# Moving the blocks of a weight tile in SBUF: two encoder layers on one Trainium2 core

## The chip, the cores and the metric

The kernel runs on one core of one Trainium2 chip. The metric is the device time of one execution in microseconds. The runs of the kernel before took 2366.05, 2366.12 and 2366.2 us; the median is 2366.12 us.

## The reference: what is computed

Two layers of a bidirectional encoder act on 272 rows (256 tokens and 16 learned meta tokens) of 2048 features, all in float32. Cut to what matters here, one layer is:

```python
proj = jnp.einsum('bld,dp->blp', h, w_in)                     # 2048 -> 6176 columns
y_gla = _gla_mixer(gq, gk, gv, gr, glr, gla_w_up, ...)        # chunkwise gated linear attention, both directions
y_na = _na_mixer(nq, nk, nv, na_rel_bias)                     # 2-D neighbourhood attention with 16 heads
mix = jnp.einsum('blm,md->bld', jnp.concatenate([y_gla, y_na], axis=-1), w_out)
h = _layer_norm(DEEPNORM_ALPHA * h + mix, ln1_w, ln1_b)
ff = jnp.einsum('blf,fd->bld', jnp.square(jax.nn.relu(jnp.einsum('bld,df->blf', h, w_ff1))), w_ff2)
h = _layer_norm(DEEPNORM_ALPHA * h + ff, ln2_w, ln2_b)        # w_ff1: 2048 -> 8192, w_ff2: 8192 -> 2048
```

The meta tokens are dropped at the end, so the second layer computes most things for 256 rows only. Nearly all arithmetic is in the four dense products with `w_in`, `w_out`, `w_ff1` and `w_ff2`.

## The kernel before, in words

**Numbers in two parts.** TensorE multiplies operands in the format fp32r, which holds less than float32. So each operand is kept as a high part (the value rounded to fp32r) and a low part (the rest). A product w·x is computed as three matmuls: high w on high x, high w on low x, low w on high x.

**Activations.** They lie with features on the 128 partitions and tokens along the free dimension, 16 tiles for x, 16 for y, and 32 for the hidden layer u (the first 16 of these reuse the place of y). `pair` makes one tile of 2 x 288 numbers for both parts. In the first layer the high part has 272 columns from the start of the tile, and the low part begins at number 288 (`PITCH`), which is 1152 bytes on. In the second layer ("dense") the two parts of 256 columns lie back to back in y and u, so that one matmul can stream both as 512 columns (`once`).

**Weights.** They come from memory in 768 tiles of 128 x 1024 numbers, each of them eight blocks of 128 x 128. `order` fixes the order of all 768, and `weights` keeps two tiles made ahead. `made` issues the load on the queue of SP, then lets ScalarE (ACT) round the tile to its high part `wh` (L180) and VectorE (DVE) subtract to get the low part `wl` (L181). Three buffers each of `raw`, `wh` and `wl` are in turn. The first tile of all is loaded and split in pieces by `head`.

**Matmuls.** `by_m` walks over the output blocks; for each it takes tiles of eight weight blocks and calls `eight`: eight times high weights on the high and on the low part (L216, 272 columns each, or L213, both parts at once as 512 columns), then eight times low weights on the high part (L219). Each matmul has its own weight load, which runs beside the matmul ahead of it. `by_k` (L246) is used in a few places where the inputs become ready one after another: it holds four or eight output banks open and gives each weight block of a tile to another of these.

**What else runs.** Attention, normalisation and evictions are generators that are stepped between weight tiles (`pump`). Their matmuls stand between those of the dense products: among them GLA's outputs (L638 to L642), whose stationary blocks are from `V` and whose streamed operand is `parts`, a tile of rows of 272 numbers.

**Addresses.** A weight tile is 4096 bytes per partition and each block of it 512 bytes. The tiles of x, y, u and the weights all begin at multiples of 256 bytes in a partition, which the unused tile `pad` of 40 numbers at the head of the constants brings about. A block of weights therefore begins at a multiple of 256 bytes from any high part, and 128 bytes off that from any low part of the first layer.

Of the kernel before, what the change touches and what calls it, by code (L numbers as in the profile page):

```python
# [7 lines left out]
F32 = mybir.dt.float32  # L8
F32R = mybir.dt.float32r
U8 = mybir.dt.uint8  # L10
AF = mybir.ActivationFunctionType
ALU = mybir.AluOpType
PSUM = bass.MemoryType.PSUM

P = 128
D = 2048
DC = D // P
T = 256
NM = 16
L = T + NM  # L20
# [6 lines left out]
WB = 1024  # L27
# [10 lines left out]
MEET = 2  # L38
PAD = 40
PITCH = 288  # L40


class Pair(tuple):


    def __new__(cls, both, dense=False):
        flat = both.rearrange("p a c -> p (a c)")
        parts = (flat[:, :T], flat[:, T:2 * T]) if dense else (both[:, 0, :], both[:, 1, :])
        made = super().__new__(cls, parts)
        made.both, made.once = both, flat[:, :2 * T] if dense else both[:, :, :T]  # L50
        return made


class Trunk:
    def __init__(self, ctx, tc, ins, out):
        self.ctx, self.tc, self.nc = ctx, tc, tc.nc
        self.i, self.out = ins, out
        self.bg, self.fg, self.credit, self.fcredit = deque(), deque(), 0, 0
        self.wants, self.due, self.late = {}, None, 0
        self.x = [None] * DC  # L60
        self.stream, self.ready = self.order(), deque()
        pool = lambda name, **k: ctx.enter_context(tc.tile_pool(name=name, **k))
        self.cp = pool("const", bufs=1)
        self.xp = pool("xhl", bufs=1)
        self.yp = pool("yhl", bufs=1)
        self.wp = pool("wst", bufs=3)
        self.jp = pool("jn", bufs=1)
        self.pm = pool("pm", bufs=4, space=PSUM)
        self.pb = pool("pb", bufs=4, space=PSUM)
# [102 lines left out]
    def made(self, ap, ends):  # L172
        if ap is None:
            return None
        nc = self.nc
        raw, wh, wl = (self.wp.tile([P, WB], d, name=nm, tag=nm)
                       for nm, d in (("raw", F32), ("wh", F32R), ("wl", F32R)))
        for c in map(slice, (0,) + ends, ends):
            nc.sync.dma_start(raw[:, c], ap[:, c])
            nc.scalar.copy(wh[:, c], raw[:, c])  # L180
            self.wl = nc.vector.tensor_tensor(wl[:, c], raw[:, c], wh[:, c].bitcast(F32), ALU.subtract).ins  # L181
        if not ends:
            self.head(ap, raw, wh, wl)
        return wh, wl

    def head(self, ap, raw, wh, wl):

        nc, q = self.nc, WB // 4
        both = self.xr.tile([P, 2, q + L], F32, name="head", tag="head", bufs=1)
        self.x[:2] = [self.pair(self.xp, "x", c) for c in range(2)]  # L190
        for c in range(2):
            nc.sync.dma_start(both[:, c], self.i["head"][:, c])
        nc.sync.dma_start(raw[:, 2 * q:], ap[:, 2 * q:])
        for c in range(2):
            at = slice(c * q, c * q + q)
            h, lo = (t[:, :L] for t in self.x[c])
            todo = [(both[:, c, q:], h, lo), (both[:, c, :q], wh[:, at], wl[:, at])]
            for args in todo[::-1] if c else todo:
                self.split(*args)
        for at in (slice(2 * q, 3 * q), slice(3 * q, WB)):  # L200
            nc.scalar.copy(wh[:, at], raw[:, at])
            self.wl = nc.vector.tensor_tensor(wl[:, at], raw[:, at], wh[:, at].bitcast(F32), ALU.subtract).ins

    def eight(self, ps, wh, wl, x, n, first, last, once):

        mm = self.nc.tensor.matmul
        c = lambda w, j: w[:, j * P:j * P + P]  # L210
        for j, v in enumerate(x):
            if once:
                mm(ps, lhsT=c(wh, j), rhs=v.once, start=first and not j, stop=False)  # L213
                continue
            for i in range(2):
                mm(ps[:, :n], lhsT=c(wh, j), rhs=v[i][:, :n], start=first and not i + j, stop=False)  # L216
        o = ps[:, T:] if once else ps[:, :n]
        for j, (h, _) in enumerate(x):
            mm(o, lhsT=c(wl, j), rhs=h[:, :T if once else n], start=False, stop=last and j == 7)  # L219
# [10 lines left out]
    def by_k(self, acts, n, before, wide=False):  # L230

        ps = [self.pm.tile([P, 512], F32, name="mm", tag="mm") for _ in range(4)]
        if wide:
            ps += [self.bank() for _ in range(4)]
        nk = len(acts)
        for k in range(0, nk, 2):
            before(k)
            for g in range(0, len(ps), 4):
                wh, wl = self.weights()
                parts = ((wh, 0), (wh, 1), (wl, 0))  # L240
                order = [(j, p, m) for j in range(2) for p in range(3) for m in range(4)]
                by_output = k == nk - 2 or k == 0 and not wide
                order.sort(key=lambda o: (o[0], o[2] // 2) if wide and not k + g else (by_output and o[2], o[1] // 2))
                for j, p, m in order:
                    c = j * 512 + m * P
                    self.nc.tensor.matmul(ps[g + m][:, :n], lhsT=parts[p][0][:, c:c + P], rhs=acts[k + j][parts[p][1]][:, :n],  # L246
                                          start=k + j + p == 0, stop=k == nk - 2 and j + p == 3)
        return [p[:, :n] for p in ps]

# [26 lines left out]

    def pair(self, pool, name, c):
        both = pool.tile([P, 2, PITCH], F32R, name=f"{name}{c}", tag=f"{name}{c}", bufs=1)
        return Pair(both, dense=name in ("y", "u") and not self.full)


    def layer(self, l):
# [91 lines left out]
    def load_gates(self):  # L374

        place = lambda c: self.yp.tile([P, 2, PITCH], F32, name=f"gw{c}", tag=f"y{c}", bufs=1).rearrange("p a c -> p (a c)")[:, :512]
        *self.wup, self.wlr = (place(c) for c in (8, 9, 10))
# [563 lines left out]
    def reuse(self, name, c, dtype):  # L941

        t = self.xp.tile([P, 2, PITCH], dtype, name=f"{name}{c}", tag=f"x{c}", bufs=1)
        return t.rearrange("p a c -> p (a c)")[:, :512]
# [235 lines left out]
```

## Time and profile before

| what | value |
|---|---|
| median of the runs | 2366.12 us |
| the profiled execution | 2366.29 us |
| its span, from the first to the last instruction | 2364.5 us |
| mean granted TensorE clock | 0.999 |
| TensorE busy | 2356.2 us (100%) |
| weight loads busy | 2241.9 us (95%) |
| VectorE busy | 1520.8 us (64%) |
| ScalarE busy | 1219.3 us (52%) |
| read from memory | 414.03 MB, 176 GB/s over the span |

"Busy" of TensorE is measured from each matmul's start to its modelled end. Matmuls overlap, since one begins while the one ahead of it still drains, so the sum of the durations in a group is more than the time in which they passed. The rate at which they follow each other is read from the timeline: the start of one group, the start of the next, and the number of matmuls between.

### The profile page before, as it was taken

What the parts mean: (1) busy time and instruction counts of PE and PEld (TensorE: products, weight loads), DVE (VectorE), ACT (ScalarE), POOL (GpSimd) and SP (SyncE); (2) the same over time, 40 slices, a digit from 0 to 9 for tenths busy, and PEclk for the clock granted to TensorE, in tenths of its full rate; (3) what the DMA queues carried; (4) which work ended last, traced back from release to release, by engine and by line L of the source; (5) the groups of instructions that cost most, each with busy time, mean ns of one, the idle gap of its engine ahead of it and who ended that gap; (6) DMA issues with size and microseconds to landing.
All of it is one profiled execution on the core that took longest, in us unless ns stands there. A gap on an engine that the chain in (4) does not pass through costs nothing.

```text
span 2364.5 us, 44607 instructions
## 1 busy us (share of the span) xinstructions
PE 2356.2 (100%) x18180; PEld 2241.9 (95%) x18180; DVE 1520.8 (64%) x2432; ACT 1219.3 (52%) x2100; POOL 136.2 (6%) x200
## 2 busy tenths in 40 slices
PE   9999999999999999999999999999999999999998
PEld 9999999999999999999999899999988888888888
DVE  5588777775544455546576787778766455666654
ACT  5666664564433344444456666655644333444443
POOL 0021100100000000000030111101100000000000
PEclk9999999999999999999999999999999999999999
DMA  7454445555555555555555555455566666556664
GB/s 261 153 160 153 156 135 176 173 176 178 177 178 176 176 177 179 177 177 174 177 184 171 164 160 165 155 160 188 187 192 190 189 187 188 188 190 212 195 188 144
DMA packets 118301, 419.02 MB, mean 177 GB/s; under 512 B 13512, under 2 KB 14024, under 8 KB 118096
## 3 DMA queue, kind: packets, MB, share of 16 engines
q1 hardware_dynamic: 117808, 415.65, 55.8%
q8 instruction: 142, 2.33, 0.4%
q14 instruction: 63, 0.52, 0.1%
q10 hardware_dynamic: 288, 0.52, 0.1%
HBM read 414.03 MB, written 2.10 MB: 176 GB/s over the span
## 4 chain that ended last, share of the span: by engine, by line
PE 98%; DVE 1%; issue 0%; ACT 0%; POOL 0%; DVEq 0%; ACTq 0%; POOLq 0%
PE mm L216 35%; PE mm L219 29%; PE mm L213 22%; PE mm L246 6%; PE bg L246 1%; PE bg L757 1%; PE mm L696 1%; PE bg L557 0%; PE bg L403 0%; DVE wl L181 0%; PE mm L722 0%; PE mm L446 0%; PE bg L883 0%; PE bg L608 0%; PE bg L638 0%
## 5 line engine op out<-in xcount | busy, mean ns | idle before, releaser
L181 DVE TENSOR_TENSOR wl<-raw,wh 128x1024 fp32r<-128x1024 f32 (+1 forms) x768 | 941.8, 1227 | 621.5 <-ACT wh L180 618.4
L180 ACT CAST wh<-raw 128x1024 fp32r<-128x1024 f32 (+1 forms) x768 | 803.5, 1047 | 919.4 <-PE mm L216 367.7
L216 PE MATMUL mm<-x,wh 128*128 128x272 f32 (+2 forms) x4224 | 569.8, 287 | 0.0
L216 PEld LDWEIGHTS mm<-x,wh 128*128 128x128 f32 x4224 | 541.1, 188 | 0.8 <-PE mm L696 0.2
L219 PE MATMUL mm<-x,wl 128*128 128x272 f32 (+3 forms) x3264 | 466.9, 285 | 0.0
L219 PEld LDWEIGHTS mm<-x,wl 128*128 128x128 f32 x3264 | 437.5, 189 | 11.6
L213 PE MATMUL mm<-x,wh 128*128 128x512 f32 x1152 | 290.1, 394 | 0.0
L213 PEld LDWEIGHTS mm<-x,wh 128*128 128x128 f32 x1152 | 207.2, 189 | 37.9 <-PE mm L696 0.4
L219 PE MATMUL mm<-y,wl 128*128 128x272 f32 (+1 forms) x1408 | 200.5, 285 | 0.0
L219 PEld LDWEIGHTS mm<-y,wl 128*128 128x128 f32 x1408 | 189.5, 189 | 6.5
L216 PE MATMUL mm<-y,wh 128*128 128x272 f32 (+1 forms) x1440 | 193.3, 286 | 0.0
L216 PEld LDWEIGHTS mm<-y,wh 128*128 128x128 f32 x1440 | 184.3, 188 | 0.0
L213 PE MATMUL mm<-y,wh 128*128 128x512 f32 x688 | 172.6, 392 | 0.0
L219 PE MATMUL mm<-u,wl 128*128 128x272 f32 (+1 forms) x1024 | 145.8, 285 | 0.0
L213 PEld LDWEIGHTS mm<-y,wh 128*128 128x128 f32 x688 | 123.6, 189 | 21.9
L219 PEld LDWEIGHTS mm<-u,wl 128*128 128x128 f32 x1024 | 137.8, 189 | 4.8
L216 PE MATMUL mm<-u,wh 128*128 128x272 f32 (+1 forms) x1056 | 141.2, 286 | 0.0
L216 PEld LDWEIGHTS mm<-u,wh 128*128 128x128 f32 x1056 | 134.9, 188 | 0.0
L213 PE MATMUL mm<-u,wh 128*128 128x512 f32 x496 | 124.2, 392 | 0.0
L213 PEld LDWEIGHTS mm<-u,wh 128*128 128x128 f32 x496 | 89.2, 189 | 15.9
L246 PE MATMUL mm<-x,wh 128*128 128x272 f32 (+1 forms) x512 | 73.3, 288 | 0.0
L246 PEld LDWEIGHTS mm<-x,wh 128*128 128x128 f32 x512 | 67.9, 191 | 0.0
(273 smaller groups left out, 1856.5 us busy)
## 6 DMA issues: line engine op xcount, KB each, us to landing
raw<-in_wff SPq DMA_DIRECT2D x512, 512.0 KB, 3.6
raw<-in_win SPq DMA_DIRECT2D x190, 512.0 KB, 3.8
raw<-in_wout SPq DMA_DIRECT2D x64, 512.0 KB, 3.6
nb<-in_nab SPq DMA_DIRECT2D x16, 352.0 KB, 4.7
xraw<-in_xT SPq DMA_DIRECT2D x7, 272.0 KB, 5.2
out<-out SPq DMA_DIRECT2D x5, 256.0 KB, 3.2
brow<-in_norm SPq DMA_DIRECT2D x4, 256.0 KB, 4.8
gw<-in_wup SPq DMA_DIRECT2D x4, 196.0 KB
```

The source lines that it names most:

```text
L180: nc.scalar.copy(wh[:, c], raw[:, c])
L181: self.wl = nc.vector.tensor_tensor(wl[:, c], raw[:, c], wh[:, c].bitcast(F32), ALU.subtract).ins
L213: mm(ps, lhsT=c(wh, j), rhs=v.once, start=first and not j, stop=False)
L216: mm(ps[:, :n], lhsT=c(wh, j), rhs=v[i][:, :n], start=first and not i + j, stop=False)
L219: mm(o, lhsT=c(wl, j), rhs=h[:, :T if once else n], start=False, stop=last and j == 7)
L246: self.nc.tensor.matmul(ps[g + m][:, :n], lhsT=parts[p][0][:, c:c + P], rhs=acts[k + j][parts[p][1]][:, :n], start=k + j + p == 0, stop=k ...
L696: nc.tensor.matmul(ps[hh][:, t * NKEY:t * NKEY + NKEY], lhsT=q[hs, NM + t * P:NM + t * P + P], rhs=k[hs, t, :], start=True, stop=True)
L757: nc.tensor.matmul(po[t][hs, :P], lhsT=v2[ts, hs] if rest else v1[:, t, hs], rhs=p2[ts, hh, :] if rest else p1[:, 2 * hh + t, :], start=re ...
```

## The change

The eight blocks of `wh` and of `wl` no longer lie back to back. Between the starts of two blocks lie 128 numbers plus a skew of 0, 8, ..., 56 numbers, that is 0 to 224 bytes of gap. The skew of a high tile is `SKEWS[(t + t // 8) % 8]` for the t-th weight tile, that of a low tile `SKEWS[t // 8 * 3 % 8]`, so 64 tiles in a row meet all 64 pairs. Each of these tiles takes 1472 numbers (5888 bytes) per partition rather than 1024. The copy of ScalarE and the subtraction of VectorE are the same, but write eight rows of 128 numbers. The low part of u in the first layer begins 1088 bytes behind its high part for u16 to u23 and 1216 bytes behind for u24 to u31, rather than 1152. The scratch space for dynamic DMAs goes from 8192 to 2048 bytes, which makes room. Numbers, order and count of the matmuls and weight loads stay as they are.

```diff
+SKEWS = (0, 8, 16, 24, 32, 40, 48, 56)
+SPAN = 1472
 class Pair(tuple):
-    def __new__(cls, both, dense=False):
+    def __new__(cls, both, dense=False, low=PITCH):
         flat = both.rearrange("p a c -> p (a c)")
-        parts = (flat[:, :T], flat[:, T:2 * T]) if dense else (both[:, 0, :], both[:, 1, :])
+        parts = (flat[:, :T], flat[:, T:2 * T]) if dense else (flat[:, :L], flat[:, low:low + L])
+        if low == PITCH and not dense:
+            parts = both[:, 0, :], both[:, 1, :]
...
-        raw, wh, wl = (self.wp.tile([P, WB], d, name=nm, tag=nm)
-                       for nm, d in (("raw", F32), ("wh", F32R), ("wl", F32R)))
+        raw = self.wp.tile([P, WB], F32, name="raw", tag="raw")
+        blocks = raw.rearrange("p (b c) -> p b c", c=P)
+        wh, wl = (self.skewed(nm, s) for nm, s in zip(("wh", "wl"), self.skew()))
         for c in map(slice, (0,) + ends, ends):
             nc.sync.dma_start(raw[:, c], ap[:, c])
-            nc.scalar.copy(wh[:, c], raw[:, c])
-            self.wl = nc.vector.tensor_tensor(wl[:, c], raw[:, c], wh[:, c].bitcast(F32), ALU.subtract).ins
+            self.halves(blocks, wh, wl, slice(c.start // P, c.stop // P))
...
+    def skew(self):
+        t = self.tiles
+        self.tiles += 1
+        return SKEWS[(t + t // 8) % 8], SKEWS[t // 8 * 3 % 8]
+
+    def skewed(self, name, skew):
+        flat = self.wp.tile([P, SPAN], F32R, name=name, tag=name)
+        return bass.AP(flat.tensor, flat.offset, [flat.ap[0], [P + skew, WB // P], [1, P]])
+
+    def halves(self, raw, wh, wl, at):
+        self.nc.scalar.copy(wh[:, at], raw[:, at])
+        self.wl = self.nc.vector.tensor_tensor(wl[:, at], raw[:, at], wh[:, at].bitcast(F32), ALU.subtract).ins
...
-        c = lambda w, j: w[:, j * P:j * P + P]
+        c = lambda w, j: w[:, j]
...
-                    c = j * 512 + m * P
-                    self.nc.tensor.matmul(ps[g + m][:, :n], lhsT=parts[p][0][:, c:c + P], rhs=acts[k + j][parts[p][1]][:, :n],
+                    self.nc.tensor.matmul(ps[g + m][:, :n], lhsT=parts[p][0][:, 4 * j + m], rhs=acts[k + j][parts[p][1]][:, :n],
...
     def pair(self, pool, name, c):
         both = pool.tile([P, 2, PITCH], F32R, name=f"{name}{c}", tag=f"{name}{c}", bufs=1)
-        return Pair(both, dense=name in ("y", "u") and not self.full)
+        low = PITCH if name != "u" else L if c < 24 else 2 * PITCH - L
+        return Pair(both, dense=name in ("y", "u") and not self.full, low=low)
...
-    nc = bacc.Bacc("TRN2", target_bir_lowering=False, num_devices=1, dynamic_dma_scratch_size=8192)
+    nc = bacc.Bacc("TRN2", target_bir_lowering=False, num_devices=1, dynamic_dma_scratch_size=2048)
```

More of the change, by code (lines that the diff above doesn't have):

```diff
@@ L60, in __init__ @@
         self.x = [None] * DC
-        self.stream, self.ready = self.order(), deque()
+        self.stream, self.ready, self.tiles = self.order(), deque(), 0
         pool = lambda name, **k: ctx.enter_context(tc.tile_pool(name=name, **k))
@@ L175, in made, with head @@
         nc = self.nc
-        raw, wh, wl = (self.wp.tile([P, WB], d, name=nm, tag=nm)
-                       for nm, d in (("raw", F32), ("wh", F32R), ("wl", F32R)))
+        raw = self.wp.tile([P, WB], F32, name="raw", tag="raw")
+        blocks = raw.rearrange("p (b c) -> p b c", c=P)
+        wh, wl = (self.skewed(nm, s) for nm, s in zip(("wh", "wl"), self.skew()))
         for c in map(slice, (0,) + ends, ends):
             nc.sync.dma_start(raw[:, c], ap[:, c])
-            nc.scalar.copy(wh[:, c], raw[:, c])
-            self.wl = nc.vector.tensor_tensor(wl[:, c], raw[:, c], wh[:, c].bitcast(F32), ALU.subtract).ins
+            self.halves(blocks, wh, wl, slice(c.start // P, c.stop // P))
         if not ends:
-            self.head(ap, raw, wh, wl)
+            self.head(ap, raw, blocks, wh, wl)
         return wh, wl
-    def head(self, ap, raw, wh, wl):
+    def skew(self):
[8 more added lines that the diff above has]
+        self.wl = self.nc.vector.tensor_tensor(wl[:, at], raw[:, at], wh[:, at].bitcast(F32), ALU.subtract).ins
+    def head(self, ap, raw, blocks, wh, wl):
         nc, q = self.nc, WB // 4
@@ L194, in head @@
         for c in range(2):
-            at = slice(c * q, c * q + q)
+            at = slice(2 * c, 2 * c + 2)
             h, lo = (t[:, :L] for t in self.x[c])
-            todo = [(both[:, c, q:], h, lo), (both[:, c, :q], wh[:, at], wl[:, at])]
+            todo = [(both[:, c, q:], h, lo), (both[:, c, :q].rearrange("p (b c) -> p b c", c=P), wh[:, at], wl[:, at])]
             for args in todo[::-1] if c else todo:
                 self.split(*args)
-        for at in (slice(2 * q, 3 * q), slice(3 * q, WB)):
-            nc.scalar.copy(wh[:, at], raw[:, at])
-            self.wl = nc.vector.tensor_tensor(wl[:, at], raw[:, at], wh[:, at].bitcast(F32), ALU.subtract).ins
+        for at in (slice(4, 6), slice(6, 8)):
+            self.halves(blocks, wh, wl, at)
     def eight(self, ps, wh, wl, x, n, first, last, once):
         mm = self.nc.tensor.matmul
-        c = lambda w, j: w[:, j * P:j * P + P]
+        c = lambda w, j: w[:, j]
         for j, v in enumerate(x):
```

## The prediction

> **What bounds the kernel now.** I read the page's busy times first, then the chain that ended last, then who waited for whom, then the groups by shape, and last the timeline of TensorE, for the distance from one matmul's start to the next. From the page:
>
> ```profile
> span 2364.5 us, 44607 instructions
> PE 2356.2 (100%) x18180; PEld 2241.9 (95%) x18180; DVE 1520.8 (64%) x2432; ACT 1219.3 (52%) x2100; POOL 136.2 (6%) x200
> PE 98%; DVE 1%; issue 0%; ACT 0%; POOL 0%; DVEq 0%; ACTq 0%; POOLq 0%
> PE mm L216 35%; PE mm L219 29%; PE mm L213 22%; PE mm L246 6%; PE bg L246 1%; PE bg L757 1%; PE mm L696 1%; PE bg L557 0%; PE bg L403 0%; DVE wl L181 0%; PE mm L722 0%; PE mm L446 0%; PE bg L883 0%; PE bg L608 0%; PE bg L638 0%
> L181 DVE TENSOR_TENSOR wl<-raw,wh 128x1024 fp32r<-128x1024 f32 (+1 forms) x768 | 941.8, 1227 | 621.5 <-ACT wh L180 618.4
> L180 ACT CAST wh<-raw 128x1024 fp32r<-128x1024 f32 (+1 forms) x768 | 803.5, 1047 | 919.4 <-PE mm L216 367.7
> ```
>
> TensorE is the chain, 98% of the span, 86% of it in three lines of one function. All its waits, from the view of waits:
>
> ```profile
> PE bg L372 <- DVE zero L369: 1.2, 1, 1.2
> PE bg L883 <- ACT sp L268: 0.7, 1, 0.7
> PE bg L883 <- DVE sp L269: 0.3, 1, 0.3
> ```
>
> That is 2.2 us, so no engine feeds it too late. The time is the number of matmuls times the pace at which one follows another. How many there are, by shape:
>
> ```profile
> L216 PE MATMUL mm<-x,wh 128*128 128x272 f32 x3584 | 483.1, 287 | 0.0
> L216 PE MATMUL mm<-y,wh 128*128 128x272 f32 x1408 | 189.1, 286 | 0.0
> L216 PE MATMUL mm<-u,wh 128*128 128x272 f32 x1024 | 137.1, 286 | 0.0
> L219 PE MATMUL mm<-x,wl 128*128 128x272 f32 x1792 | 260.3, 287 | 0.0
> L219 PE MATMUL mm<-y,wl 128*128 128x272 f32 x704 | 102.3, 287 | 0.0
> L219 PE MATMUL mm<-u,wl 128*128 128x272 f32 x512 | 74.4, 287 | 0.0
> L213 PE MATMUL mm<-x,wh 128*128 128x512 f32 x1152 | 290.1, 394 | 0.0
> L213 PE MATMUL mm<-y,wh 128*128 128x512 f32 x688 | 172.6, 392 | 0.0
> L213 PE MATMUL mm<-u,wh 128*128 128x512 f32 x496 | 124.2, 392 | 0.0
> L219 PE MATMUL mm<-x,wl 128*128 128x256 f32 x1152 | 160.4, 282 | 0.0
> L219 PE MATMUL mm<-y,wl 128*128 128x256 f32 x704 | 98.2, 282 | 0.0
> L219 PE MATMUL mm<-u,wl 128*128 128x256 f32 x512 | 71.4, 282 | 0.0
> ```
>
> 6016 matmuls with high weights over 272 columns, 3008 with low weights over 272, 2336 over 512 and 2368 over 256. The durations overlap; the pace is in the timeline of TensorE (first column: start in us):
>
> ```profile
> 821.73 2.14 PE L216 MATMUL mm<-u,wh 128*128 128x272 f32 x16
> 823.71 1.16 PE L219 MATMUL mm<-u,wl 128*128 128x272 f32 x8
> 824.71 2.14 PE L216 MATMUL mm<-u,wh 128*128 128x272 f32 x16
> 1900.92 2.00 PE L213 MATMUL mm<-u,wh 128*128 128x512 f32 x8
> 1902.76 1.12 PE L219 MATMUL mm<-u,wl 128*128 128x256 f32 x8
> 1903.71 2.00 PE L213 MATMUL mm<-y,wh 128*128 128x512 f32 x8
> ```
>
> One tile of layer 0 takes 16 matmuls in 1.98 us (123.8 ns each), then 8 in 1.00 us (125 ns). One of layer 1 takes 8 in 1.84 us (230 ns), then 8 in 0.95 us (118.8 ns). The grouped durations lie 162 ns above these paces (286 against 123.8, 392 against 230), so a duration in the other rows is read as a pace by taking 162 off. Times counts, the four groups make 744.5 + 376.0 + 537.3 + 281.2 = 1939 us of the span.
>
> **Part 1: weight blocks at other distances.** Nothing is added or removed on TensorE: the same matmuls and weight loads stand in the same order. What changes is the address at which a weight block begins against the operand that streams past. Before, every weight block, every high part and every second-layer low part begins at a multiple of 256 bytes from the others; a low part of x, y or u in layer 0 lies 1152 bytes behind its high part, so 128 bytes off. After, the high tile takes one of eight distances by its number and the low tile another, by its number over 8. In the built program the high-weight matmuls over 272 columns, half of them at 0 and half at 128 before, then stand at 0 and 128 in about a quarter of the cases each, and at 32, 64, 96, 160, 192, 224 in the rest. One tile in eight keeps its old distance, so 7/8 of the matmuls of by_m can change pace.
>
> Does the trace hold matmuls at such distances? The GLA outputs do: their streamed operand (parts) has rows of 1088 bytes and starts 160 past a multiple of 256, and V blocks lie at 512, so the distances there are 32, 96, 160 and 224. The first row and the row after the last of seven plus seven of them over 272 columns, and the same over 256:
>
> ```profile
> 145.54 0.28 PE L638 MATMUL bg<-parts,V 128*128 128x272 f32 x1
> ...
> 147.30 0.91 PE L216 MATMUL mm<-x,wh 128*128 128x272 f32 x6
> ```
>
> ```profile
> 1506.60 0.28 PE L639 MATMUL bg<-parts,V 128*128 128x256 f32 x1
> ...
> 1508.14 1.04 PE L216 MATMUL mm<-x,wh 128*128 128x272 f32 x7
> ```
>
> 14 matmuls in 1.76 us are 125.7 ns each; 13 in 1.54 us are 118.5 ns each. And those of by_k in layer 0, at 0 and 128 but four in a row with one operand:
>
> ```profile
> 26.43 2.18 PE L246 MATMUL bg<-x,wh 128*128 128x272 f32 x16
> 28.44 1.17 PE L246 MATMUL bg<-x,wl 128*128 128x272 f32 x8
> ```
>
> 16 in 2.01 us, 125.6 ns. So 125.6 to 125.7 is the pace over 272 columns wherever the steady exchange of a high and a low part at 0 and 128 is missing, whatever the distances. That exchange is the one row that is quicker (123.8), and the change breaks it in seven tiles of eight. I take 125.7.
>
> The sum, each count times 7/8: high weights over 272, 6016 x 7/8 x (125.7 - 123.8) = +10.0 us; low weights over 272, 3008 x 7/8 x (125.7 - 125.0) = +1.8 us; over 256, 2368 x 7/8 x (118.5 - 118.8) = -0.6 us. Over 512 columns no other distance is in the trace. Its bounds are the quickest and slowest undisturbed rows of that line, and those of the other two lines stand beside it (minimum, median, maximum in ns):
>
> ```profile
> L213 PE MATMUL mm<-u,wh x496: 389/391/398, 1819.9 to 2338.6; 128*128 128x512 f32 x166
> L216 PE MATMUL mm<-u,wh x1056: 283/288/290, 642.9 to 2350.3; 128*128 128x272 f32 x171, 128*128 128x256 f32 x5
> L219 PE MATMUL mm<-u,wl x1024: 277/284/296, 644.9 to 2351.2; 128*128 128x272 f32 x86, 128*128 128x256 f32 x85
> ```
>
> The mean of 392 lies near the minimum, 3 ns above 389 and 6 below 398, so most of these run in the line's quick state; the x rows at 394 carry 320 matmuls whose streamed operand has a gap of 128 bytes in its middle. I take half the way to x, +1 ns: 2336 x 7/8 x 1 = +2.0 us. The remaining matmuls (L246, small ones) are left at their rows. Sum: +13 us.
>
> **Part 2: low part of u.** It lies 1088 bytes behind the high part for u16 to u23, 1216 for u24 to u31, 64 bytes off the old 1152 either way. Only the 1024 high-weight matmuls on u over 272 columns see it, and only the tiles with unmoved weights are not yet counted: 1024 / 8 x 1.9 ns = 0.2 us.
>
> **Part 3: the split.** ACT's copy and DVE's subtraction now run over 8 rows of 128 instead of one of 1024. Per tile they are 1047 and 1227 ns; DVE is idle for 621.5 us before its 768, ACT for 919.4, so each could grow by 0.8 us per piece before it set the pace. Cost nil, hidden beside the 2.8 to 3.0 us that TensorE spends on a tile; without the cover a tenth more per piece would be 94 us of DVE time. Bounds: zero below, a few tenths of a microsecond above, in the first 50 us where TensorE follows the loads. The scratch space that shrinks from 8192 to 2048 bytes moves all tiles by 6144 bytes, a multiple of 256, and no queue of the page uses it: nil.
>
> **The sum.** 2366.3 us for the profiled execution (0.2 above the median of 2366.1) + 13 + 0.2 = 2379; I say 2380. Lower end, every line at the minima above (216: 283, low weights over 272: 283, low weights over 256: 277, 512 columns: 389): 7/8 x (-3.3 x 6016 - 4 x 3008 - 5 x 2368 - 3 x 2336) = -44 us, 2322. Upper end, at the 290 of L216, 4 ns on the low weights (L416's mean below), 3 ns over 256, 398 over 512: 7/8 x (4 x 6016 + 4 x 3008 + 3 x 2368 + 6 x 2336) = +50 us, 2416.
>
> ```profile
> L416 PE MATMUL bg<-lr,up 98*128 98x272 f32 x16 | 3.4, 291 | 0.0
> L403 PE MATMUL bg<-x,ws 128*64 128x272 f32 x32 | 8.1, 286 | 0.0
> ```
>
> L416 (distance 64) and L403 (32 and 160, with a shorter weight load) are the other rows at such distances: one worse, one like today's.
>
> **The rivals.** *Faster:* the two streams collide most where their blocks stand in step, and the spread takes them apart. For it: pace differs by address at all (283 to 290 in one shape). Against it: the GLA rows at spread distances are no quicker. It would give L216 a pace of 121 (its quicker half), low weights 121, 512 columns 227: 7/8 x (-2.8 x 6016 - 4 x 3008 - 3 x 2336) = -31 us, 2335. It decides once the mean over 272 columns falls under 123.8 ns. Chance 0.27.
>
> *No difference:* the streams don't disturb each other, the spread of durations is pipeline jitter, and the address does nothing: 2366. Against it stands the regularity of the rows above: by_m's 123.8 and by_k's 125.6 differ only in order and address. Chance 0.11. The Trainium skill has this as a rule: TensorE: Matmul & The Clock Gate, Step-by-step, says that two independent read ports let the next weights load without taking from the running matmul, and SBUF — State Buffer, Who interferes with whom, that TensorE waits on no one. By it the sum would be 2366 instead of 2380; the trace here leans against it.
>
> *Worse than forecast:* some of the 64 pairings run at the slow rows (290, 398) and nothing falls back into step, so the mean goes half-way to the upper end, +25 us and more, 2391 to 2416. For it: L416 and the 134 ns steps inside L219 (296). Chance 0.17.
>
> The first of those pages, Wait — 56ns, not 53.3ns?, gives N/2.4 + 2.5 ns for a warm matmul, 116 ns over 272 columns and 216 over 512; as an estimate by that, the most a perfect layout could give is some 75 us over 272 and 33 over 512. No row of this kernel runs at it.
>
> **How the numbers follow.** The forecast, 2380 (2371 to 2391), has 0.45. A measurement of this kernel tells about 0.2% from no change, 4.7 us. Faster by more: the first rival, 0.27, and a hair of the jitter. Within: the second and the lowest end of the forecast, 0.13. Slower: 0.60. The range of 8 in 10 reaches from the faster rival's 2335 to 2412, just inside the upper end.
>
> **What would show it.** TensorE still at 98% of the chain and the waits still near 2 us: then only pace moved. L216 (L232 after) over 272 columns near 288 instead of 286.5, L219 (L235) over 272 near 287.5, over 256 unchanged, L213 (L229) near 394. Wrong if the 272 groups fall under 286, or if DVE or ACT shows up as a releaser of TensorE.

## The result and the profile after

The changed kernel takes 2376.82 us in the median (2376.53 to 2376.88), the kernel before 2366.16 us over the runs of both rounds. The ratio is 1.0043, with a 95% interval of 1.0029 to 1.0057: slower by 10.7 us. The profiled execution has a span of 2375.0 us against 2364.5 us, 10.5 us more, and the clock is the same (1.00).

From the page of the kernel after, its busy line and the engines of its chain, and from its view of waits, everything that TensorE waited for:

```profile
PE 2366.8 (100%) x18180; PEld 2247.2 (95%) x18180; DVE 1520.0 (64%) x2432; ACT 1219.2 (51%) x2100; POOL 135.6 (6%) x200
PE 99%; DVE 0%; DMA 0%; ACT 0%; issue 0%; SPq 0%; DVEq 0%; ACTq 0%
```

```profile
PE bg L388 <- DVE zero L385: 1.2, 1, 1.2
PE bg L899 <- ACT sp L283: 0.7, 1, 0.7
PE bg L899 <- DVE sp L284: 0.3, 1, 0.3
```

TensorE is still the whole chain, the counts are the same, and its waits are the same 2.2 us. The split on VectorE and ScalarE takes what it took (1520.0 and 1219.2 us). So all of the 10.5 us is pace. The groups by shape of the kernel after, in the order of the prediction's (L232 is L216 of before, L235 is L219, L229 is L213):

```profile
L232 PE MATMUL mm<-x,wh 128*128 128x272 f32 x3584 | 487.5, 288 | 0.0
L232 PE MATMUL mm<-y,wh 128*128 128x272 f32 x1408 | 191.1, 288 | 0.0
L232 PE MATMUL mm<-u,wh 128*128 128x272 f32 x1024 | 138.7, 288 | 0.0
L235 PE MATMUL mm<-x,wl 128*128 128x272 f32 x1792 | 261.4, 288 | 0.0
L235 PE MATMUL mm<-y,wl 128*128 128x272 f32 x704 | 102.8, 288 | 0.0
L235 PE MATMUL mm<-u,wl 128*128 128x272 f32 x512 | 74.8, 288 | 0.0
L229 PE MATMUL mm<-x,wh 128*128 128x512 f32 x1152 | 291.9, 395 | 0.0
L229 PE MATMUL mm<-y,wh 128*128 128x512 f32 x688 | 173.9, 394 | 0.0
L229 PE MATMUL mm<-u,wh 128*128 128x512 f32 x496 | 125.2, 394 | 0.0
L235 PE MATMUL mm<-x,wl 128*128 128x256 f32 x1152 | 159.6, 281 | 0.0
L235 PE MATMUL mm<-y,wl 128*128 128x256 f32 x704 | 97.5, 281 | 0.0
L235 PE MATMUL mm<-u,wl 128*128 128x256 f32 x512 | 71.0, 281 | 0.0
```

The first number after the bar is the busy time of a group, and its difference to before is where the time went: high weights over 272 columns 4.4 + 2.0 + 1.6 = +8.0 us; low weights over 272 +1.1 + 0.5 + 0.4 = +2.0 us; over 512 columns +1.8 + 1.3 + 1.0 = +4.1 us; over 256 columns -0.8 - 0.7 - 0.4 = -1.9 us. That is +12.2 us; the other groups give 1.7 us back, by_k 0.8 of it.

The timeline of TensorE of the kernel after shows the pace of single tiles:

```profile
815.12 2.17 PE L232 MATMUL mm<-u,wh 128*128 128x272 f32 x16
817.12 1.16 PE L235 MATMUL mm<-u,wl 128*128 128x272 f32 x8
1913.15 2.02 PE L229 MATMUL mm<-y,wh 128*128 128x512 f32 x8
1915.00 1.10 PE L235 MATMUL mm<-y,wl 128*128 128x256 f32 x8
```

These two pairs are the first and the second layer. Sixteen high-weight matmuls in 2.00 us are 125 ns each, where it was 123.8; eight over 512 columns in 1.85 us are 231 ns (230 before).

### The profile page after: what moved, and what is told of

It reads as the page before. It is cut to its first block, busy times and chain, and to the rows that moved or that the text cites. A ratio compares the mean times of both kernels' runs of the same rounds, so it can differ in the third digit from the quotient of the medians.

```text
span 2375.0 us, 44607 instructions
## 1 busy us (share of the span) xinstructions
PE 2366.8 (100%) x18180; PEld 2247.2 (95%) x18180; DVE 1520.0 (64%) x2432; ACT 1219.2 (51%) x2100; POOL 135.6 (6%) x200
## 4 chain that ended last, share of the span: by engine, by line
PE 99%; DVE 0%; DMA 0%; ACT 0%; issue 0%; SPq 0%; DVEq 0%; ACTq 0%
PE mm L232 35%; PE mm L235 29%; PE mm L229 23%; PE mm L261 6%; PE bg L261 1%; PE bg L773 1%; PE mm L712 1%; PE bg L573 1%; PE bg L419 0%; PE mm L738 0%; DMA raw<-in_win 0%; PE mm L462 0%; PE bg L899 0%; PE bg L624 0%; PE bg L654 0%; PE bg L628 0%
## 5 line engine op out<-in xcount | busy, mean ns | idle before, releaser
L200 ACT CAST wh<-raw 128x1024 fp32r<-128x1024 f32 (+1 forms) x770 | 804.4, 1045 | 936.8 <-PE mm L232 427.2
L232 PE MATMUL mm<-x,wh 128*128 128x272 f32 (+2 forms) x4224 | 573.8, 288 | 0.0
L232 PEld LDWEIGHTS mm<-x,wh 128*128 128x128 f32 x4224 | 544.3, 188 | 0.8 <-PE mm L712 0.2
L235 PE MATMUL mm<-x,wl 128*128 128x272 f32 (+3 forms) x3264 | 467.3, 285 | 0.0
L235 PEld LDWEIGHTS mm<-x,wl 128*128 128x128 f32 x3264 | 437.8, 188 | 12.6
L229 PE MATMUL mm<-x,wh 128*128 128x512 f32 x1152 | 291.9, 395 | 0.0
L229 PEld LDWEIGHTS mm<-x,wh 128*128 128x128 f32 x1152 | 206.6, 188 | 39.0 <-PE mm L712 0.4
L235 PE MATMUL mm<-y,wl 128*128 128x272 f32 (+1 forms) x1408 | 200.2, 284 | 0.0
L235 PEld LDWEIGHTS mm<-y,wl 128*128 128x128 f32 x1408 | 189.2, 188 | 7.4
L232 PE MATMUL mm<-y,wh 128*128 128x272 f32 (+1 forms) x1440 | 195.2, 287 | 0.0
L232 PEld LDWEIGHTS mm<-y,wh 128*128 128x128 f32 x1440 | 185.8, 188 | 0.0
L229 PE MATMUL mm<-y,wh 128*128 128x512 f32 x688 | 173.9, 394 | 0.0
L235 PE MATMUL mm<-u,wl 128*128 128x272 f32 (+1 forms) x1024 | 145.8, 285 | 0.0
L229 PEld LDWEIGHTS mm<-y,wh 128*128 128x128 f32 x688 | 123.2, 188 | 22.5
L235 PEld LDWEIGHTS mm<-u,wl 128*128 128x128 f32 x1024 | 137.7, 188 | 5.4
L232 PE MATMUL mm<-u,wh 128*128 128x272 f32 (+1 forms) x1056 | 142.8, 288 | 0.0
L232 PEld LDWEIGHTS mm<-u,wh 128*128 128x128 f32 x1056 | 136.3, 188 | 0.0
L229 PE MATMUL mm<-u,wh 128*128 128x512 f32 x496 | 125.2, 394 | 0.0
L229 PEld LDWEIGHTS mm<-u,wh 128*128 128x128 f32 x496 | 88.9, 188 | 16.5
```

Of the source, the lines that this page charges most:

```text
L200: self.nc.scalar.copy(wh[:, at], raw[:, at])
```

## The experiments

Three theories were set against each other. **Theory 1**, the prediction's: a matmul and the weight load beside it fall into a steady exchange; what costs is that the change breaks it, and the distances as such cost the same. **Theory 2**: each distance has a fixed price, whatever came before. **Theory 3** was formed after the fifth run: each distance of the streamed operand from the weight block, counted modulo 256 bytes and held constant, settles at a pace of its own; a mixture costs about the mean over them, and the state in which a tile is entered can decide which of several steady patterns it falls into.

### No skew, but the rest of the change

```diff
-SKEWS = (0, 8, 16, 24, 32, 40, 48, 56)
+SKEWS = (0,) * 8
```

> All skews are zero; the longer weight tiles and the new places of the low parts of u stay. Both theories expect no loss from the tiles' pitch of 5888 bytes (a multiple of 256): 2366 us, and only the 1024 matmuls of high weights on u can move, by at most 2 ns each, so 2365 to 2368. If it comes out at 2375 or more, the loss has nothing to do with the skews but with the tile's pitch or with u.

Measured: 2369.02 us (2368.27 to 2370.38), 1.0011 of before (1.0002 to 1.0021). Every large group equals its row of before to 0.1 us but one:

```profile
L232 PE MATMUL mm<-u,wh 128*128 128x272 f32 x1024 | 139.3, 288 | 0.0
```

That was 137.1 us. So the tile's pitch costs nothing, and the other place of u's low part costs 2.2 us by itself, about the 2 ns a matmul that were expected as the most (the time is 1 us above the range of 2365 to 2368): high weights on low parts at 1088 or 1216 bytes go slower than at 1152.

### Only the high tiles skewed

```diff
-        return SKEWS[(t + t // 8) % 8], SKEWS[t // 8 * 3 % 8]
+        return SKEWS[(t + t // 8) % 8], 0
```

(u as before the change, here and in the next one.)

> Only the high weight tiles are skewed; the low tiles have their blocks back to back, and u is as before. Theory 1 (what costs is that the steady exchange of matmul and weight load is lost; the distances as such cost the same): high weights over 272 columns go from 124.2 to 125.5 ns (+8 us) and over 512 from 230.8 to 232.5 (+4 us), and the unmoved low weights move too, since they are entered in another state: 125.0 to 125.6 over 272, 119.0 to 118.2 over 256; together 2376 to 2378. Theory 2 (every distance has a fixed price): the high ones as above, the low ones stay at 125.0 and 119.0: 2378.

Measured: 2376.36 us (2375.99 to 2377.14), 1.0042 of before (1.0027 to 1.0057), nearly all of the change's loss. Two of its groups:

```profile
L232 PE MATMUL mm<-x,wh 128*128 128x272 f32 x3584 | 486.7, 288 | 0.0
L235 PE MATMUL mm<-x,wl 128*128 128x272 f32 x1792 | 261.0, 288 | 0.0
```

High weights on x rise by 3.6 us over 272 columns (483.1 before), as both theories said. The low weights, whose distances are those of before, rise by 0.7 us on x (260.3 before). That is less than theory 1 said and more than theory 2. Over 256 columns the low weights stay (160.3 us on x, 160.4 before), as theory 2 said. The run as a whole does not tell the two apart.

### Only the low tiles skewed

```diff
-        return SKEWS[(t + t // 8) % 8], SKEWS[t // 8 * 3 % 8]
+        return 0, SKEWS[t // 8 * 3 % 8]
```

> Only the low weight tiles are skewed; the high tiles have their blocks back to back and u is as before, so all high weights stand at their old distances. Theory 2 (a fixed price for each distance): high weights keep 124.2 ns over 272 columns and 230.8 over 512; low ones move by +0.6 and -0.8; sum 2366, within 2 us. Theory 1 (the exchange falls into one of several steady patterns according to the state in which it is entered): many high tiles fall into the slower pattern although their distances are the old ones, the mean over 272 goes to about 125 and over 512 to about 232, 2372 to 2376.

Measured: 2370.79 us (2369.81 to 2372.11), 1.0019 of before (1.0009 to 1.0028). Between the two expectations, and the rows say why. High weights, none of which was moved:

```profile
L232 PE MATMUL mm<-x,wh 128*128 128x272 f32 x3584 | 485.5, 287 | 0.0
L232 PE MATMUL mm<-y,wh 128*128 128x272 f32 x1408 | 190.7, 287 | 0.0
L229 PE MATMUL mm<-x,wh 128*128 128x512 f32 x1152 | 290.2, 394 | 0.0
```

Over 272 columns they lose 2.4 us on x, 1.6 on y and 0.9 on u, together 4.9; a fixed price for each distance (theory 2) can't do that. Over 512 they stay, which theory 1 did not expect. The timeline shows it tile by tile. The first rows are a tile whose low blocks have no skew, the others two tiles in a row whose low blocks have 96 bytes:

```profile
846.90 2.14 PE L232 MATMUL mm<-x,wh 128*128 128x272 f32 x16
848.88 1.16 PE L235 MATMUL mm<-x,wl 128*128 128x272 f32 x8
...
858.83 2.17 PE L232 MATMUL mm<-x,wh 128*128 128x272 f32 x16
860.83 1.17 PE L235 MATMUL mm<-x,wl 128*128 128x272 f32 x8
861.84 2.15 PE L232 MATMUL mm<-x,wh 128*128 128x272 f32 x16
863.82 1.17 PE L235 MATMUL mm<-x,wl 128*128 128x272 f32 x8
```

The same sixteen matmuls at the same distances take 1.98 us (846.90 to 848.88), 2.00 (858.83 to 860.83) and 1.98 (861.84 to 863.82), and it goes on in turn. After its first few matmuls a quick tile has starts 121 and 126 ns apart in turn in the trace; the slow one shown has 125, 128, 123 and 124, again and again, and slow tiles behind a skew of 64 bytes 123, 123, 125 and 129. Which it is depends on the low blocks ahead: of the tiles of this kind, all but a few behind skews of 0 or 32 bytes (82 of 84) are quick, and all but a few (130 of 135) behind 64, 128 or 160 bytes are slow; behind 96 and 224 bytes they change in turn, and behind 192 most are quick (26 of 35).

### A scan of skew and of the low part's place, over 272 columns

A kernel of matmuls alone, with the addresses of the weight and activation tiles as in the kernel; its core, shortened:

```python
for j in range(8):
    for i in range(2):
        mm(ps[:, :272], lhsT=at(wh, j * (128 + skew)), rhs=at(x, j * 576 + i * low), ...)
for j in range(8):
    mm(ps[:, :272], lhsT=at(wl, j * (128 + skew)), rhs=at(x, j * 576), ...)
```

> A kernel of matmuls alone, whose output is zeros: it leaves the whole computation of the reference out. 64 series of six weight tiles each, with the pattern of the first layer (eight blocks, high and low part over 272 columns, then eight over 272). Each series has one skew for high and low blocks (0 to 224 bytes) and one distance of low to high part (1088 to 1312 bytes). Theory 1: in step, the pace depends weakly on the pairing; the series with no skew and 1152 bytes repeats 123.7 ns for the first sixteen, the others lie between 122 and 127, mostly 125 to 126. Theory 2: single pairings stand out by several ns, down to 116 to 119 or up to 130.

From the starts of the matmuls in its trace, with the first two tiles of each series left out, a tile takes 2980 to 3060 ns over the 64 series, 3013 in the middle. The two quickest are no skew with 1152 bytes, that is the kernel before, and 32 bytes with 1216; both have 2980. The repeated pattern of the first is the 121, 126 of the kernel. Its groups, with those of the second slowest (64 bytes and 1248, 3053 ns a tile):

```profile
L44 PE MATMUL tac<-x,wh 128*128 128x272 f32 x96 | 12.9, 286 | 0.0
L44 PE MATMUL tcf<-x,wh 128*128 128x272 f32 x96 | 13.2, 290 | 0.0
```

So matmuls alone reproduce the kernel's pace, without any work on the other engines beside them: 2980 ns a tile, where the kernel has 2.98 us. No pairing stands out by the 5% that theory 2 allowed, and the first layer stood at the best of these 64 already.

### A scan for the second layer, and runs at one distance

```python
mm(ps[:cols, :n], lhsT=at(wh, k % 8 * 128, cols), rhs=at(x, distance + k % 8 * 576), ...)   # 64 times
```

> Again matmuls alone; the output is zeros and the whole computation of the reference is left out. First 64 series with the pattern of the second layer (eight matmuls over 512 columns, eight over 256), each with one skew for the high and one for the low blocks. Then runs of 64 matmuls at one constant distance (0 to 224 bytes) for 272, 256 and 512 columns, with the usual weight block of 128 columns and, at three distances, with a block of only 32 columns. Theory 1: the series with no skew repeats 2793 ns a tile, the others lie within 1% of it (2770 to 2820); the constant runs lie at 124 to 127 ns over 272 columns whatever the distance. Theory 2: single pairings or distances stand apart by 3% and more. On what the streams do to each other: if a weight load beside a matmul slows it, the runs with 32 columns of weights are quicker, by 5 ns or more over 272 columns and by 8 or more over 512; if the load does not touch the matmul, the 512 columns take the same 227 to 230 ns with the short load.

The core of the runs at one distance, shortened, stands above. The 64 series with skews, in the second layer's pattern, take 2773 to 2847 ns a tile, 2793 with no skew; theory 1's range, with one outlier above. The runs at one distance say more. From its timeline (m: 272 columns, k: 256, v: 512; the letters a to h are distances of 0 to 224 bytes in steps of 32; an x in the middle is a block of 32 columns of weights):

```profile
1109.42 8.18 PE L56 MATMUL ma<-x,wh 128*128 128x272 f32 x64
1117.45 8.21 PE L56 MATMUL mb<-x,wh 128*128 128x272 f32 x64
...
1149.81 8.06 PE L56 MATMUL mf<-x,wh 128*128 128x272 f32 x64
1157.71 8.06 PE L56 MATMUL mg<-x,wh 128*128 128x272 f32 x64
...
1173.63 7.83 PE L56 MATMUL ka<-x,wh 128*128 128x256 f32 x64
1181.29 7.71 PE L56 MATMUL kb<-x,wh 128*128 128x256 f32 x64
...
1219.16 7.42 PE L56 MATMUL kg<-x,wh 128*128 128x256 f32 x64
1226.42 7.73 PE L56 MATMUL kh<-x,wh 128*128 128x256 f32 x64
1233.98 14.72 PE L56 MATMUL va<-x,wh 128*128 128x512 f32 x64
1248.54 15.10 PE L56 MATMUL vb<-x,wh 128*128 128x512 f32 x64
1263.47 14.82 PE L56 MATMUL vc<-x,wh 128*128 128x512 f32 x64
...
1352.85 8.12 PE L56 MATMUL mxa<-x,wh 128*32 128x272 f32 x64
1360.82 8.09 PE L56 MATMUL mxc<-x,wh 128*32 128x272 f32 x64
1368.74 8.10 PE L56 MATMUL mxe<-x,wh 128*32 128x272 f32 x64
1376.68 7.42 PE L56 MATMUL kxa<-x,wh 128*32 128x256 f32 x64
1383.93 7.42 PE L56 MATMUL kxc<-x,wh 128*32 128x256 f32 x64
1391.19 7.42 PE L56 MATMUL kxe<-x,wh 128*32 128x256 f32 x64
1398.45 14.99 PE L56 MATMUL vxa<-x,wh 128*32 128x512 f32 x64
1413.28 15.00 PE L56 MATMUL vxc<-x,wh 128*32 128x512 f32 x64
1428.12 14.96 PE L56 MATMUL vxe<-x,wh 128*32 128x512 f32 x64
```

The difference of two starts over 64 is the pace. Over 256 columns it is 119.7 ns at distance 0 (ka) and 113.4 at 192 bytes (kg). Over 512 it is 227.5 at distance 0 (va) and 233.3 at 32 bytes (vb). Over 272 it is 125.5 at 0 and 123.4 at 160 (mf). So theory 1 falls in one point: a constant distance has a pace of its own, up to 5.6% apart. Averaged over all eight, from ma to ka, from ka to va and from va to mxa over 512 matmuls each, the paces are 125.4, 117.9 and 232.2 ns. The mixed kernel has 125.6, 118.2 and 232.5 for high weights over 272, low ones over 256, and 512 columns (means of the steps between starts in its trace). Mixing gave about the mean.

The kernel does not have all eight equally often. By its skews, of 64 weight blocks 20 stand at 0 bytes from a high part, 12 at 128, 8 each at 64 and 192, and 4 at each of the other four distances. Weighted like this (half of the high weights over 272 columns counted 128 bytes on, for the low part), the constant runs give 125.6, 118.2 and 231.0 ns. So over 272 and 256 columns the mean holds to 0.1 ns, while over 512 the kernel is 1.5 ns slower than it. The run va has 232.0 ns in the mean over its first seven steps and 226.7 over its last forty; that eight matmuls in a row are too few to settle would fit, but is not shown.

The short weight block answers the other question in part. Its loads take 108 to 109 ns each instead of 188. By the same reading, with the full block at the same distances (0, 64 and 128 bytes) in brackets, the pace is 113.3, 113.4 and 113.4 ns over 256 columns (119.7, 117.8, 118.8), 124.5, 123.8 and 124.1 over 272 (125.5, 126.7, 126.7), and 231.7, 231.9 and 231.1 over 512 (227.5, 229.1, 233.3). So it is quicker by 4.4 to 6.4 ns over 256 columns and by 1.0 to 2.9 over 272, and slower at two of three distances over 512. Neither branch of the expectation holds: nothing gains 5 ns over 272 or 8 over 512, and 512 columns do not stay at 227 to 230. With the short block the distance hardly matters any more (0.8 ns at most between the three, against up to 5.8), so the weight block takes part in setting the pace. It also has only 32 output rows, so this run does not show that it is the length of the load that does it.

### A scan of shifts, and the low tiles shifted in the kernel

Here the blocks lie back to back, and whole tiles are shifted, so that a matmul's distance is constant while the address of the streamed operand stays:

```diff
+SHIFT = 16
+SPAN = 1088
...
-        return SKEWS[(t + t // 8) % 8], SKEWS[t // 8 * 3 % 8]
+        return 0, SHIFT
...
-        return bass.AP(flat.tensor, flat.offset, [flat.ap[0], [P + skew, WB // P], [1, P]])
+        return bass.AP(flat.tensor, flat.offset + skew, [flat.ap[0], [P, WB // P], [1, P]])
```

These lines are from the run in the kernel: each low tile is shifted by 16 numbers, 64 bytes, and u is as before the change. The scan adds the shifts to the addresses of its blocks in the same way. A weight tile shifted by 64 bytes has the streamed operand at 192 bytes from it, modulo 256, so it corresponds to the constant run at 192.

> Matmuls alone, with zeros for an output and the reference's computation left out. Blocks lie back to back, but the whole high tile and the whole low tile are shifted by 0 to 224 bytes each, so every matmul of a kind has one constant distance: 64 series with the pattern of the first layer (low part at 1152 bytes), then 64 with that of the second. Theory 3, from the constant runs of the scan before (each constant distance has a steady pace of its own, and mixing gives their mean): low weights shifted by 64 bytes take 114 to 117 ns over 256 columns instead of 119.0, and with unshifted high weights (226.7 to 230 over 512) the second layer's tile takes 2755 to 2775 ns instead of 2793; the other shifts of the high weights give 2800 or more. Theory 1 (distances cost the same, only the change between them costs): all series within 10 ns of 2793.

In the second layer's pattern the 64 series take 2746 to 2827 ns a tile. No shift gives 2793; the quickest has the high tile at 192 bytes and the low one at 64, with 229.4 ns over 512 columns and 114.0 over 256. With the high tile unshifted and the low one at 64 it is 2780, above the 2755 to 2775 expected: its eight low matmuls take 117.9 ns, and if their pace in the 64-long run is the settled one, eight are too few to settle. In the first layer's pattern the series take 2973 to 3029 ns, no shift 2980; the best, the high tile at 96 bytes and the low one at 96 or 192, gain 7 ns a tile, which was not tried in the kernel.

The scan also bears on a question that the runs at one distance leave open. They moved the streamed operand, so its own start moved too; here it stays and the weights move. Yet the order is the same. Averaged over the eight shifts of the other tile, low weights are quickest at a shift of 64 (115.5 ns, the others 117.6 to 119.5), the distance of 192 that is quickest in the constant runs. The 512 columns are quickest at high shifts of 0 and 192 (230.2 and 230.4, the others 232.5 to 233.4), the distances of 0 and 64 that are quickest there (227.5 and 229.1, the others 233.3 to 234.4). That speaks for the distance between the two, and not the address of either.

> The kernel before, but each low weight tile begins 64 bytes later in a longer buffer (one constant distance for all matmuls of a kind, no skew, u as before). Theory 3: 2368 low-weight matmuls over 256 columns go from 119.0 to 114 to 117 ns (-5 to -12 us), 3008 over 272 columns from 125.0 to 123.5 to 125 (0 to -5 us), the high ones keep 124.2 and 230.8 if they are still entered in the quick pattern: 2350 to 2362 us. Should the entry turn to the slow pattern, 6016 times 0.8 to 1.3 ns come on top: 2355 to 2369. Theory 1: 2366, as nothing varies from tile to tile.

Measured in the kernel: 2362.34 us (2361.36 to 2363.64), 0.9982 of before (0.9973 to 0.9991). At the upper edge of theory 3's range (2350 to 2362), below theory 1's 2366.

```profile
L235 PE MATMUL mm<-x,wl 128*128 128x256 f32 x1152 | 159.1, 281 | 0.0
```

The low weights over 256 columns gain 1.3 us on x (160.4 before) and 2.8 us on x, y and u together, where 5 to 12 were expected; the trace has 117.6 ns a step, not 114 to 117. Over 272 columns the gain of up to 5 us that was hoped for is not there: low weights have 125.4 ns a step, 125.1 before. What fills the gap is that the high weights, which were expected to stay, gain 1.6 us over 272 columns and 1.0 over 512. So the time is at the edge of the range, but its terms are not those of theory 3.

### Shifts in the second layer alone

```diff
+SHIFTS = ((0, 0), (48, 16))
...
+        return SHIFTS[t // 384]
```

> The first layer's 384 weight tiles lie as in the kernel before; in the second layer each high tile is shifted by 192 bytes and each low tile by 64. Theory 3 (constant distances have paces of their own, read from the scan of shifts: 2746 ns a tile instead of 2793): some 250 tiles of the second layer gain 47 ns each, -12 us, with 512 columns near 229.4 and 256 columns near 114 to 116 ns; 2353 to 2358 us. If the scan does not carry over to the kernel, where other matmuls stand between the tiles, 2360 to 2366.

Measured: 2352.09 us (2351.4 to 2353.26), 0.9938 of before (0.9924 to 0.9951). That is 14 us better than before, better than either kernel, and 1 us below the range of 2353 to 2358. Its timeline in the second layer:

```profile
1892.06 1.07 PE L235 MATMUL mm<-y,wl 128*128 128x256 f32 x8
1892.97 2.00 PE L229 MATMUL mm<-u,wh 128*128 128x512 f32 x8
1894.81 1.07 PE L235 MATMUL mm<-u,wl 128*128 128x256 f32 x8
```

Eight matmuls over 256 columns take 0.91 us, 113.8 ns each, where it was 118.8; 512 columns keep 230. A tile takes 2.75 us instead of 2.79. The first layer's tiles lie as they did. The scan carried over to the kernel: over the whole trace the mean step is 114.6 ns over 256 columns (119.1 before) and 230.2 over 512 (230.8 before).

## Why the prediction was right or wrong

The forecast of 2380 us against 2376.8 was right in sign and near in size. The misses of its terms cancel in part (-2.0, +0.2, -1.3 and +2.1 us for the four groups in the order below, and -1.7 for the other groups, which were left at their rows), so the nearness is luck to that extent. Point by point:

- **The bound and the waits**: as forecast. TensorE is the chain, and its waits are the same 2.2 us.
- **High weights over 272 columns**: +10.0 forecast, +8.0 measured. The price, the pace of matmuls outside the exchange (125.7), was taken from the GLA outputs and by_k; the scan's mean over eight constant distances is 125.4 and the mixed kernel has 125.6. That a few rows at odd distances spoke for all eight was luck in part: the constant runs span 123.4 to 126.7, and only 8 of the 14 GLA rows have their blocks in V (L638 and L639; L640 and L642 take theirs from y and VS). That the pace is the same whatever the distance, once the exchange is broken, is wrong.
- **Which tiles pay**: the step "7/8 of the matmuls" failed. The tiles with unmoved blocks were taken to keep their pace; the run with skewed low tiles alone shows that a tile at its old distances goes slower when it is entered from another low tile (+4.9 us). The losses do not add: low alone costs 4.4 us, high alone 10.0, u alone 2.6, all together 10.7.
- **Low weights**: over 272 +1.8 forecast, +2.0 measured. Over 256 -0.6 forecast, -1.9 measured: distance 0, where they stood, is one of the two slowest of eight (119.7 ns; the mean is 117.9), so the step from 118.8 to the 118.5 of the GLA rows was too small.
- **512 columns**: +2.0 forecast, +4.1 measured, the largest miss. Half the way to the x rows was too little: the kernel before stood at the quickest of eight distances (227.5 ns in a constant run), and the mean lies at 232.2.
- **u**: 0.2 us beside part 1, 2.2 us when done alone. In the whole change it is nearly swallowed: u's group of high weights over 272 columns takes 138.7 us in it, and 138.3 in the run with the high tiles skewed and u as before.
- **The split**: nil, as forecast; 1047 and 1227 ns a tile became 1045 and 1224.
- **The rivals**: *faster* falls, as over 272 and 512 columns the spread cost and only over 256 it gained. *No difference* falls: a constant shift of the weights alone moves the time by 14 us. *Worse than forecast* falls: the large groups have means of 288 ns over 272 columns and 394 to 395 over 512, not near the slow rows of 290 and 398. The Trainium skill's rule (TensorE: Matmul & The Clock Gate, Step-by-step) that loading the next weights takes no SBUF read bandwidth from the running matmul is not borne out as a rule for the pace: the same full load goes at 227.5 or 233.3 ns by its distance, and over 256 columns the short load is quicker by 4.4 to 6.4 ns, though over 512 it is slower at two of three distances. Whether read bandwidth is the reason, no run here shows. And the N/2.4 + 2.5 of that page of the Trainium skill (Wait — 56ns, not 53.3ns?) was not reached by any series or constant run of the scans: the best is 113.3 over 256 columns, where it gives 109 as an estimate.

## What to carry to other kernels

Where TensorE's pace is the whole time, the address of the stationary block against the streamed operand is worth a scan: matmuls alone, in the order of the kernel, reproduce the kernel's pace to about a nanosecond a matmul, and the best of the constant shifts carried over for a gain of 0.6%. A mixture of distances gives about the mean over them, so it loses to a good constant one. Judge a layout on whole tiles in their order, as the start of a tile depends on how the one ahead of it ended.

## What the runs showed of the hardware

- A row of equal matmuls settles into a repeating pattern of steps between starts, and more than one exists for the same distances (121, 126; 125, 128, 123, 124; 123, 123, 125, 129). Which one a tile of sixteen falls into goes with the layout of the low weights ahead of it: 1.98 us behind a skew of 0 or 32 bytes, 2.00 to 2.01 behind 64, 128 or 160.
- Over 256 columns a constant distance of 192 bytes goes at 113.4 ns, distance 0 at 119.7; over 512 columns it is distance 0 that is quick (227.5 against up to 234.4).
- A block of 32 instead of 128 columns of weights goes at 113.3 to 113.4 ns over 256 columns, 123.8 to 124.5 over 272 and 231.1 to 231.9 over 512 at the three distances tried, so with it most of the effect of the distance is gone. What makes the pace depend on the weight block stays open: no run here shows which resource it is.
- As far as these runs go, it is the distance that orders the paces, whether the streamed operand moves (the runs at one distance) or the weights do (the scan of shifts). No run moved both together, and each scan was run once.
